# Hybrid RWKV-7 / GLA / SSD stack on one core: modulation weights summed over row tiles by VectorE alone, 1024 columns at a time

## The chip, the cores and the metric

The kernel runs on one core of a Trainium2 chip. The metric is device time in microseconds (us) of one execution. TensorE (PE) multiplies matrices into PSUM, VectorE (DVE) does elementwise work on two sources, ScalarE (ACT) does activations and copies, GpSimd (POOL) and SyncE (SP) mostly issue DMAs. Each engine takes its instructions in the order in which they stand in its queue, and they wait for each other through semaphores.

## The reference

Four layers (RWKV-7, GLA, SSD, RWKV-7) act on 256 tokens of width 2048, in float32. Each layer has a modulation: a vector-matrix product of `silu(c)` (2048) with a 2048 x 6144 matrix, whose result is split into shift, scale and gate. The change touches only how this product is computed.

```python
c_act = jax.nn.silu(c)
for i in range(DEPTH):                                   # DEPTH = 4, kinds 0, 1, 2, 0
    mod = jnp.einsum('bd,de->be', c_act, ada_w[i]) + ada_b[i]
    shift, scale, gate = jnp.split(mod[:, None, :], 3, axis=-1)
    h = rms_normalize(x, norm_g[i], NORM_EPS) * (1 + scale) + shift
    out = mixer(h)                                       # rwkv7_mixer, gla_mixer or ssd_mixer
    x = x + (gate * out)
return rms_normalize(x, final_g, NORM_EPS)
```

The four matrices `ada_w` are 201 MB in float32, and each element is used once.

## The kernel before, in words

**The projections.** All large matrix products go through `jobs` (L333). A job is one weight tile `raw` of 128 x 1024 float32 (512 KB: 4 row tiles of 256 columns), loaded by SP's queue. ScalarE casts it to a rounded part H (L312), VectorE subtracts to get the rest L (L314), and TensorE does 24 matmuls of 128 x 256 with them (L367). There are 6 `raw` buffers, 3 of H and 3 of L. The program has 706 such tiles.

**The modulation.** It runs beside the projections, as a Python generator (`ada_all`, L227) that is advanced a step at a time. A step of `ada_group` (L259) loads one 512 KB tile of `ada_w` (two row tiles of 512 columns) into the same six `raw` buffers. There are 8 steps to a group, 4 groups to a third (shift, scale or gate) and 3 thirds to a layer: 384 steps. A group needs, for its 512 columns, the sum over 2048 rows of `c_act[row] * w[row, column]`. It is formed in two ways at once: a step whose flag in `share` is 1 is multiplied by TensorE (L277, eight matmuls per step, each 32 identical columns of `c_act` against 128 columns, at four places of the array), and a step whose flag is 0 is added by VectorE into `adaacc`, one instruction per row tile of 512 columns (L283; the first one is ScalarE's, L281). At the group's end, matmuls with ones (L287) sum `adaacc` over its 128 partitions on top of that, and a copy and a small matmul (L290, L291) turn the row into a column. `SHARE` gives TensorE 4 steps of 8, `FEW` 2, `LEAST` 1; layers set the pattern as they go.

**When the steps come.** The 64 steps of layer 0's shift and scale come first, since nothing can start without them. After that `tick` (L369) is called after each job and advances the generator to where `PACE` says, at most 2 steps at a time, and not while `hold` is set (from the last columns of a layer's output projection into the next layer). Where a layer needs a third that is not done, `ada_need` (L299) advances the generator until it is.

**What sets the order.** A scheduler sorts each engine's instructions when the program is built, by priority and a model of time; the queues then run in that fixed order. SP's queue issues nearly all weight tiles, of `ada_w` and of the projections, in one order.

Of the kernel before, what the change touches and what calls it, by code (L numbers as in the profile page):

```python
# [9 lines left out]
F32 = mybir.dt.float32  # L10
# [3 lines left out]
ALU = mybir.AluOpType  # L14

P = 128
D = 2048
T = 256
DT = D // P
# [75 lines left out]

PACE = ((0, 120, 316, 484, 620), (0, 96, 240, 288, 320))

SHARE = (1, 0, 1, 0, 1, 0, 1, 0)
FEW = (1, 0, 0, 0, 1, 0, 0, 0)
LEAST = (1, 0, 0, 0, 0, 0, 0, 0)  # L100

# [30 lines left out]
class Kern:  # L132
    def __init__(self, ctx, tc, A, out, layers=(0, 1, 2, 3), final=True):
# [15 lines left out]
        self.hold = False  # L149
        self.share = SHARE  # L150
        self.par = self.const.tile([P, NPAR], F32, name="par")
# [75 lines left out]
    def ada_all(self):  # L227


        for i in self.layers:  # L230
# [8 lines left out]
            for q in range(3):  # L239
                if (i, q) in self.mods:  # L240
                    continue
                for n in range(4):
                    yield from self.ada_group(i, q, n, ms[q])
                if q == 1:
                    self.norm_gain(i, ms[q], 0, DT)
                self.mods[(i, q)] = ms[q]
# [12 lines left out]
    def ada_group(self, i, q, n, m):  # L259

        nc = self.nc
        wv = Weights((0, 512, self.A["ada_w"][i]))
        n0 = q * D + n * 512
        kc = RAWC // 512
        ps = acc = None
        share = self.share
        for b in range(DT // kc):
            raw = self.wpool.tile([P, kc, 512], F32, name="raw")
            nc.sync.dma_start(out=raw, in_=wv(kc * b, kc, n0, 512))
            for u in range(kc):  # L270
                k = kc * b + u
                if share[b]:
                    start = ps is None
# [5 lines left out]
                elif acc is None:  # L279
                    acc = self.adap.tile([P, 512], F32, name="adaacc")  # L280
                    nc.scalar.mul(out=acc, in_=raw[:, u, :], mul=self.cact[:, k:k + 1])  # L281
                else:
                    nc.vector.scalar_tensor_tensor(out=acc, in0=raw[:, u, :], scalar=self.cact[:, k:k + 1], in1=acc,  # L283
                                                   op0=ALU.mult, op1=ALU.add)
            yield
        for e in range(4 if acc is not None else 0):
            nc.tensor.matmul(ps[32 * e:32 * e + 32, 0:P], self.c("one", 0, 1).broadcast_to([P, 32]),  # L287
                             acc[:, e * P:(e + 1) * P], start=False, stop=True)
        s = self.adap.tile([P, P], F32, name="adas")
        nc.scalar.copy(out=s, in_=ps[:, 0:P])  # L290
        nc.tensor.matmul(ps[:, P:P + 4], s, self.c("sel4"), start=True, stop=True)  # L291
        nc.vector.tensor_tensor(out=m[:, 4 * n:4 * n + 4], in0=ps[:, P:P + 4],
                                in1=self.p("ada_b", 48 * i + 16 * q + 4 * n, 4), op=ALU.add)

    def ada_tick(self, n=1):
# [205 lines left out]
    def _rwkv(self, i, j):  # L501
# [130 lines left out]
        nc.gpsimd.dma_start(out=x[:, :, 1:], in_=xd)  # L632
        if i != self.layers[-1]:
            self.share = LEAST
        def ev(jj, ps):
# [6 lines left out]
        with ExitStack() as ctx:  # L642
            nb, = self.banks(ctx, f"pn{i}", nb=2)
            self.share = FEW if i != self.layers[-1] else SHARE
            un = 0
# [120 lines left out]
    def rwkv_second(self, i, j, un, spill, kept, rb, last):  # L766
# [110 lines left out]
        rs = self.rsqrt_tiny(mu, 1.0 / H, GN_EPS, rb)  # L877
        Y = rb.tile([P, 8, H], F32, name="Y")
        nc.vector.tensor_tensor(out=Y, in0=y8, in1=rs.unsqueeze(2).broadcast_to([P, 8, H]), op=ALU.mult)
# [150 lines left out]
    def _gla(self, i, ctx):  # L1030
# [3 lines left out]
        C, NCH = 64, 4  # L1034
        self.share = FEW
        hs = self.norm_parts(i)
# [172 lines left out]
    def _ssd(self, i):  # L1209
# [3 lines left out]
        NH, C = 64, 128  # L1213
        self.share = SHARE
        hs = self.norm_parts(i)
# [46 lines left out]
    def ssd_group(self, g, hs, win, acd, tk, due):  # L1262
# [66 lines left out]
        nc.tensor.matmul(ps, bk, xd.rearrange("p h d -> p (h d)"), start=True, stop=True)  # L1329
        st = su.tile([P, 8, 64], F32, name="st", bufs=1)  # L1330
        nc.scalar.copy(out=st.rearrange("p h d -> p (h d)"), in_=ps)
# [72 lines left out]
def host_inputs(inp):  # L1404
    w = {n: np.asarray(a) for n, a in inp.items()}
    a = {n: blocks(w[n], T, 4) for n in ("rwkv_w_in", "rwkv_w_out", "gla_w_out", "ssd_w_out")}
    a["ada_w"] = blocks(w["ada_w"], 512, 2)
    for n in ("rwkv_dec_w1", "rwkv_iclr_w1"):
# [32 lines left out]
```

## Time and profile before

| what | value |
|---|---|
| median of 3 runs | 2909.22 us (2904.7 to 2921.3) |
| the profiled execution | 2918.82 us |
| its span, first to last instruction | 2916.8 us |
| PE busy | 2782.8 us (95%) |
| DVE busy | 2116.8 us (73%) |
| ACT busy | 1397.7 us (48%) |
| DMA | 673.82 MB, mean 231 GB/s |
| mean granted clock of TensorE | 0.963 |

A busy time is the union of an engine's instructions, waits excluded. The rows further below cut the span into stretches: 0 to 146 us is the start (layer 0's shift and scale, and its first projection); 146 to 511 us the rest of the value projection, the key projection and most of the receptance projection of layer 0; 511 to 736 us its gate projection, with the state update running beside it; 736 to 890 us its output projection; 890 to 1409 us the GLA layer; 1409 to 2117 us the SSD layer, cut at 1522 us; 2117 to 2917 us the last RWKV layer and the end. The cuts are read from when L314 works on which weights.

### The profile page before, as it was taken

What the parts mean: (1) busy time and instruction counts of PE and PEld (TensorE: products, weight loads), DVE (VectorE), ACT (ScalarE), POOL (GpSimd) and SP (SyncE); (2) the same over time, 40 slices, a digit from 0 to 9 for tenths busy, and PEclk for the clock granted to TensorE, in tenths of its full rate; (3) what the DMA queues carried; (4) which work ended last, traced back from release to release, by engine and by line L of the source; (5) the groups of instructions that cost most, each with busy time, mean ns of one, the idle gap of its engine ahead of it and who ended that gap; (6) DMA issues with size and microseconds to landing.
All of it is one profiled execution on the core that took longest, in us unless ns stands there. A gap on an engine that the chain in (4) does not pass through costs nothing.

```text
span 2916.8 us, 66210 instructions
## 1 busy us (share of the span) xinstructions
PE 2782.8 (95%) x27138; PEld 2584.9 (89%) x27138; DVE 2116.8 (73%) x4000; ACT 1397.7 (48%) x2355; POOL 154.2 (5%) x298
## 2 busy tenths in 40 slices
PE   6889999999999999998999999999889999999997
PEld 4789888989898899997999999999779989899997
DVE  5778876667787867777888786887577876565675
ACT  3465564423335543444654454544357656442333
POOL 0010110100100000000000000000001111010010
PEclk8899899999999999999999999999999988999999
DMA  9877768866775777876876666666556765675553
GB/s 349 299 271 259 240 215 276 297 223 224 237 268 195 265 259 273 291 261 211 292 253 222 223 219 222 217 204 223 169 171 222 229 183 176 198 275 172 168 178 112
DMA packets 239135, 673.82 MB, mean 231 GB/s; under 512 B 72272, under 2 KB 78416, under 8 KB 235760
## 3 DMA queue, kind: packets, MB, share of 16 engines
q1 hardware_dynamic: 217904, 580.84, 60.0%
q0 software_dynamic: 20928, 88.75, 8.6%
q8 instruction: 213, 3.49, 0.5%
q14 instruction: 90, 0.74, 0.1%
HBM read 620.66 MB, written 48.82 MB: 230 GB/s over the span
## 4 chain that ended last, share of the span: by engine, by line
PE 76%; DMA 5%; DVE 5%; issue 1%; ACT 1%; SPq 1%; POOL 0%; DVEq 0%; ACTq 0%; POOLq 0%
PE acc L367 58%; PE g L762 2%; PE mx L277 2%; DMA raw<-in_ada_w 2%; DMA rv<-rd 1%; DVE L L314 1%; PE b L869 1%; PE b L846 1%; PE b L868 1%; PE b L841 1%; PE b L791 1%; DMA sp<-yd 1%; PE b L694 1%; PE b L996 1%; PE b L982 1%
## 5 line engine op out<-in xcount | busy, mean ns | idle before, releaser
L367 PE MATMUL acc<-xs,H 128*128 128x256 f32 x8480 | 1640.3, 291 | 16.7 <-ACT xs L382 6.4
L367 PEld LDWEIGHTS acc<-xs,H 128*128 128x128 f32 x8480 | 1355.3, 195 | 59.8 <-issue 21.5
L367 PE MATMUL acc<-xs,L 128*128 128x256 f32 x4240 | 1226.5, 290 | 8.6 <-DVE L L314 8.6
L312 ACT CAST H<-raw 128x1024 fp32r<-128x1024 f32 (+1 forms) x706 | 718.5, 1018 | 947.3 <-PE acc L367 688.8
L314 DVE TENSOR_TENSOR L<-raw,H 128x1024 fp32r<-128x1024 f32 (+1 forms) x706 | 835.8, 1185 | 339.4 <-ACT H L312 321.7
L367 PEld LDWEIGHTS acc<-xs,L 128*128 128x128 f32 x4240 | 824.9, 195 | 22.1 <-DVE L L314 10.2
L283 DVE SCALAR_TENSOR_TENSOR adaacc<-raw,cact,adaacc 128x512 f32<-128x512 f32 x418 | 312.5, 748 | 133.7 <-DMA raw<-in_ada_w 118.3
L367 PE MATMUL acc<-ys,H 128*128 128x256 f32 x1536 | 290.3, 288 | 2.7 <-ACT ys L382 1.9
L367 PEld LDWEIGHTS acc<-ys,H 128*128 128x128 f32 x1536 | 240.8, 192 | 14.4 <-issue 10.2
L367 PE MATMUL acc<-ys,L 128*128 128x256 f32 x768 | 219.2, 286 | 0.0
L367 PEld LDWEIGHTS acc<-ys,L 128*128 128x128 f32 x768 | 146.5, 191 | 3.2 <-issue 3.2
L277 PE MATMUL mx<-raw,cact 128*32 128x128 f32 x2416 | 115.4, 295 | 15.6 <-DMA raw<-in_ada_w 14.9
L405 DVE SCALAR_TENSOR_TENSOR x<-acc,mod,x 128x256 f32<-128x256 f32 x192 | 84.2, 480 | 52.3 <-PE acc L367 51.8
L525 ACT ACTIVATE hn<-x,mod,omu 128x256 f32<-128x256 f32 x192 | 113.0, 599 | 4.0 <-DVE xm L528 2.6
L277 PEld LDWEIGHTS mx<-raw,cact 128*32 128x32 f32 x2416 | 64.7, 114 | 42.5 <-DMA raw<-in_ada_w 13.0
L367 PE MATMUL acc<-H,xs 128*128 128x256 f32 x512 | 97.3, 290 | 0.0
L528 DVE SCALAR_TENSOR_TENSOR xm<-x,par,hn 128x256 f32<-128x256 f32 x192 | 88.3, 478 | 1.3 <-ACT hn L525 0.3
L367 PEld LDWEIGHTS acc<-H,xs 128*128 128x128 f32 x512 | 82.4, 197 | 1.2 <-issue 1.2
L762 PE MATMUL g<-abkp 64*128 64x128 f32 x768 | 72.0, 296 | 2.8 <-DVE abkp L784 2.6
L367 PE MATMUL acc<-L,xs 128*128 128x256 f32 x256 | 73.6, 289 | 0.0
L762 PEld LDWEIGHTS g<-abkp 64*128 64x128 f32 x768 | 55.0, 189 | 17.6 <-issue 8.2
L1257 DVE SCALAR_TENSOR_TENSOR cva<-cvp,hcw,cva 128x256 f32<-128x256 f32 x144 | 64.8, 480 | 0.0
(350 smaller groups left out, 3182.3 us busy)
## 6 DMA issues: line engine op xcount, KB each, us to landing
raw<-in_ada_w SPq DMA_DIRECT2D x384, 512.0 KB, 5.0
raw<-in_rwkv_w_in SPq DMA_DIRECT2D x256, 512.0 KB, 4.9
raw<-in_ssd_w_in SPq DMA_DIRECT2D x128, 512.0 KB, 4.6
raw<-in_gla_w_in SPq DMA_DIRECT2D x96, 512.0 KB, 4.7
raw<-in_ssd_w_out SPq DMA_DIRECT2D x64, 512.0 KB, 4.1
raw<-in_rwkv_w_out SPq DMA_DIRECT2D x48, 512.0 KB, 3.8
abkp<-kd POOLq DMA_DIRECT2D x16, 1024.0 KB, 7.3
raw<-in_gla_w_out SPq DMA_DIRECT2D x32, 512.0 KB, 4.9
```

Source lines behind the costliest of these rows:

```text
L277: nc.tensor.matmul(ps[32 * e:32 * e + 32, 0:P], self.cact[:, k:k + 1].broadcast_to([P, 32]), raw[:, u, e * P:(e + 1) * P], start=start, st ...
L283: nc.vector.scalar_tensor_tensor(out=acc, in0=raw[:, u, :], scalar=self.cact[:, k:k + 1], in1=acc, op0=ALU.mult, op1=ALU.add)
L312: nc.scalar.copy(out=hi, in_=raw[:, a:a + n])
L314: nc.vector.tensor_tensor(out=lo, in0=raw[:, a:a + n], in1=hi, op=ALU.subtract)
L367: self.nc.tensor.matmul(ps, lhs, rhs, start=first and part == 0 and w is hi, stop=last and w is lo)
L405: nc.vector.scalar_tensor_tensor(out=self.x[:, t, 1:], in0=ps[:, u, :], scalar=gate[:, t:t + 1], in1=self.x[:, t, 1:], op0=ALU.mult, op1=A ...
L525: nc.scalar.activation(t1, x[:, k, 1:], AF.Identity, scale=self.omu[:, col:col + 1], bias=self.mods[(i, 0)][:, k:k + 1])
L528: done[k] = nc.vector.scalar_tensor_tensor(out=xm, in0=x[:, k, 0:T], scalar=self.p("rwkv_mu", col), in1=t1, op0=ALU.mult, op1=ALU.add)
L694: nc.tensor.matmul(ps[:, q * T:(q + 1) * T], w2[0:LORA, n, q * P:(q + 1) * P], lora[nm][0:LORA], start=True, stop=True)
L762: self.nc.tensor.matmul(ps[h][:, n * C:(n + 1) * C], s[r, q, c * C:(c + 1) * C], t[r, q, c * C:(c + 1) * C], start=True, stop=True)
L791: nc.tensor.matmul(ps[:, q * T:(q + 1) * T], self.c("blk"), rT[:, q, :], start=True, stop=True)
L1257: nc.vector.scalar_tensor_tensor(out=a, in0=src[:, k:k + T], scalar=w[k], in1=a, op0=ALU.mult, op1=ALU.add)
```

## The change

Layer 0's shift and scale (64 steps) stay as they were, always with the pattern `SHARE`. The other ten thirds go through a new function, `ada_third`. It takes 1024 columns at a time, so a third is 2 halves instead of 4 groups. A step is still one 512 KB tile, now one row tile of 1024 columns. All 16 row tiles are added into a 128 x 1024 `adaacc`: the first by ScalarE, the other 15 by VectorE, one instruction each. TensorE only sums the result over partitions, once per 1024 columns, with four matmuls of 256 columns. `FEW` and `LEAST` are gone. The tile is loaded one step before ScalarE's first use of it. `PACE` has new points: no step between tick 0 and tick 60, 16 steps by tick 78, 96 by tick 150, and about the old pace from tick 319 on. Two small buffers are shared with others (`Y = s8`, `st = xd`). The matrices lie in memory in the new order of tiles.

```diff
-PACE = ((0, 120, 316, 484, 620), (0, 96, 240, 288, 320))
+PACE = ((0, 60, 78, 150, 319, 530, 660), (0, 0, 16, 96, 234, 292, 320))
 SHARE = (1, 0, 1, 0, 1, 0, 1, 0)
-FEW = (1, 0, 0, 0, 1, 0, 0, 0)
-LEAST = (1, 0, 0, 0, 0, 0, 0, 0)
...
-                for n in range(4):
-                    yield from self.ada_group(i, q, n, ms[q])
+                yield from self.ada_third(i, q, ms[q])
...
+    def ada_third(self, i, q, m):
+        nc = self.nc
+        for g in range(2):
+            acc = self.adap.tile([P, 1024], F32, name="adaacc")
+            for k in range(DT):
+                raw = self.wpool.tile([P, RAWC], F32, name="raw")
+                nc.sync.dma_start(out=raw, in_=self.A["ada_w"][3 * i + q - 2, g, k])
+                if k == 0:
+                    yield
+                    nc.scalar.mul(out=acc, in_=raw, mul=self.cact[:, k:k + 1])
+                else:
+                    nc.vector.scalar_tensor_tensor(out=acc, in0=raw, scalar=self.cact[:, k:k + 1], in1=acc,
+                                                   op0=ALU.mult, op1=ALU.add)
+                if 0 < k < DT - 1:
+                    yield
+            ps = self.bank()
+            for e in range(4):
+                nc.tensor.matmul(ps[32 * e:32 * e + 32, 0:T], self.c("one", 0, 1).broadcast_to([P, 32]),
+                                 acc[:, e * T:(e + 1) * T], start=True, stop=True)
+            s = self.adap.tile([P, T], F32, name="adas")
+            nc.scalar.copy(out=s, in_=ps[:, 0:T])
+            ps = self.bank()
+            for j in range(2):
+                nc.tensor.matmul(ps[:, j:j + 7:2], s[:, j * P:(j + 1) * P], self.c("sel4"), start=True, stop=True)
+            nc.vector.tensor_tensor(out=m[:, 8 * g:8 * g + 8], in0=ps[:, 0:8],
+                                    in1=self.p("ada_b", 48 * i + 16 * q + 8 * g, 8), op=ALU.add)
+            yield
...
-        Y = rb.tile([P, 8, H], F32, name="Y")
+        Y = s8
...
-        st = su.tile([P, 8, 64], F32, name="st", bufs=1)
+        st = xd
...
-    a["ada_w"] = blocks(w["ada_w"], 512, 2)
+    a["ada_w0"] = blocks(w["ada_w"][0:1, :, :2 * D], 512, 2)
+    n = w["ada_w"].shape[0]
+    thirds = w["ada_w"].reshape(n, D, 3, D).transpose(0, 2, 1, 3).reshape(3 * n, D, D)[2:]
+    a["ada_w"] = blocks(thirds, 1024, 1)
```

Two places in the built programs show what moves. Line numbers in the second rows of each pair are those of the changed kernel: its L298 is the load of `ada_w` (L269 before), L304 the VectorE addition (L283), L340 the cast's rest (L314), L348 the load of projection weights (L322), L431 the residual update (L405).

SP's queue at the end of layer 0's output projection, before the change; `in_gla_low` is the first tile of the next layer:

```order
L322 DMA raw<-in_rwkv_w_out 128x512
L269 DMA raw<-in_ada_w 128x1024
L322 DMA raw<-in_rwkv_w_out 128x512 x2
L269 DMA raw<-in_ada_w 128x1024
L322 DMA raw<-in_rwkv_w_out 128x512
L269 DMA raw<-in_ada_w 128x1024
L322 DMA raw<-in_rwkv_w_out 128x512
L269 DMA raw<-in_ada_w 128x1024
L322 DMA raw<-in_rwkv_w_out 128x512 x2
L322 DMA raw<-in_gla_low 128x4x16
```

The same place of the same queue after the change:

```order
L348 DMA raw<-in_rwkv_w_out 128x512
L298 DMA raw<-in_ada_w 128x1024
L348 DMA raw<-in_rwkv_w_out 128x512
L298 DMA raw<-in_ada_w 128x1024 x2
L348 DMA raw<-in_rwkv_w_out 128x512
L298 DMA raw<-in_ada_w 128x1024
L348 DMA raw<-in_rwkv_w_out 128x512
L298 DMA raw<-in_ada_w 128x1024
L348 DMA raw<-in_rwkv_w_out 128x512
L298 DMA raw<-in_ada_w 128x1024 x8
L348 DMA raw<-in_gla_low 128x4x16
```

Eight tiles of `ada_w` now stand in one piece between the last weights of layer 0 and the first of layer 1. Over the whole output projection (from its first weight row to `in_gla_low`) there are 29 tiles of `ada_w` before and 52 after, beside 40 of its own in both.

VectorE at the end of the same stretch before the change, from the last residual updates (L405) to the start of the norm (L1012 to L1020, the inverse root of the mean square):

```order
L405 SCALAR_TENSOR_TENSOR x<-acc,mod_2_88,x 128x256 x2
L314 TENSOR_TENSOR L<-raw,H 128x1024
L405 SCALAR_TENSOR_TENSOR x<-acc,mod_2_88,x 128x256 x2
L321 MEMSET raw 128x4x112
L314 TENSOR_TENSOR L<-raw,H 128x1024
L1012 TENSOR_SCALAR rsv<-nb 128x2
L1013 TENSOR_SCALAR rst<-rsv 128x2
L1015 TENSOR_SCALAR rsr<-rst 128x2
L1018 TENSOR_TENSOR rst<-rsr 128x2
L1019 SCALAR_TENSOR_TENSOR rst<-rst,rsv 128x2
```

The same place on VectorE after the change, where the norm is L1035 to L1043:

```order
L304 SCALAR_TENSOR_TENSOR adaacc<-raw,cact,adaacc 128x1024
L431 SCALAR_TENSOR_TENSOR x<-acc,mod_2_88,x 128x256 x2
L304 SCALAR_TENSOR_TENSOR adaacc<-raw,cact,adaacc 128x1024 x2
L1035 TENSOR_SCALAR rsv<-nb 128x2
L304 SCALAR_TENSOR_TENSOR adaacc<-raw,cact,adaacc 128x1024
L1036 TENSOR_SCALAR rst<-rsv 128x2
L304 SCALAR_TENSOR_TENSOR adaacc<-raw,cact,adaacc 128x1024
L347 MEMSET raw 128x4x112
L1038 TENSOR_SCALAR rsr<-rst 128x2
L304 SCALAR_TENSOR_TENSOR adaacc<-raw,cact,adaacc 128x1024
L1041 TENSOR_TENSOR rst<-rsr 128x2
```

The steps of the norm, which stood next to each other, now stand between additions that each wait for a tile to land.

## Rows read from the trace of the kernel before

**Rows 1.** Page: busy time of each engine, share of the span, instructions
```profile
PE 2782.8 (95%) x27138; PEld 2584.9 (89%) x27138; DVE 2116.8 (73%) x4000; ACT 1397.7 (48%) x2355; POOL 154.2 (5%) x298
```

**Rows 2.** Windows by stage: length, then busy us (instructions) of PE, PEld, DVE, ACT, POOL
```profile
146.00:511.00 365.00, 346.46 (x4382) 316.72 (x4375) 276.33 (x557) 212.66 (x404) 39.13 (x78) 0.95 0.76 252
511.00:736.00 225.00, 221.62 (x2063) 204.50 (x2062) 149.44 (x279) 80.22 (x137) 22.19 (x41) 0.97 0.72 250
736.00:890.00 154.00, 148.68 (x1326) 136.90 (x1324) 123.09 (x235) 58.56 (x101) 10.21 (x19) 0.99 0.74 243
890.00:1409.00 519.00, 497.93 (x4238) 459.01 (x4241) 382.40 (x629) 246.94 (x378) 2.18 (x4) 0.97 0.74 252
1409.00:1522.00 113.00, 113.00 (x1071) 105.24 (x1072) 96.63 (x192) 59.46 (x92) 1.06 (x2) 1.00 0.79 276
1522.00:2117.00 595.00, 586.89 (x5187) 562.92 (x5186) 446.01 (x826) 282.37 (x409) 5.10 (x9) 0.99 0.65 214
2117.00:2917.00 800.00, 758.89 (x7818) 711.03 (x7816) 547.72 (x1095) 394.52 (x716) 74.12 (x142) 0.96 0.59 189
```

**Rows 3.** The same windows, line L277 alone: busy us of PE and PEld
```profile
146.00:511.00 365.00, 22.62 (x440) 11.80 (x432) 0.95 0.76 252
511.00:736.00 225.00, 5.15 (x128) 3.00 (x128) 0.97 0.72 250
736.00:890.00 154.00, 4.90 (x112) 2.75 (x112) 0.99 0.74 243
890.00:1409.00 519.00, 19.49 (x436) 10.93 (x440) 0.97 0.74 252
1409.00:1522.00 113.00, 7.75 (x160) 3.99 (x160) 1.00 0.79 276
1522.00:2117.00 595.00, 17.97 (x416) 10.23 (x416) 0.99 0.65 214
2117.00:2917.00 800.00, 12.64 (x224) 6.51 (x224) 0.96 0.59 189
```

**Rows 4.** PE's timeline around one step on L277: start, duration, count
```profile
1103.40 0.28 PE L367 MATMUL acc<-L,xs 128*128 128x256 f32 x1
1103.61 0.64 PE L277 MATMUL mx<-raw,cact 128*32 128x128 f32 x16
1104.18 0.50 PE L367 MATMUL acc<-H,xs 128*128 128x256 f32 x2
```

**Rows 5.** Groups on VectorE: count | busy us, mean ns | idle before, its releasers
```profile
L314 DVE TENSOR_TENSOR L<-raw,H 128x1024 fp32r<-128x1024 f32 (+1 forms) x706 | 835.8, 1185 | 339.4 <-ACT H L312 321.7 <-PE acc L367 5.5 <-PE pv L367 4.2
L283 DVE SCALAR_TENSOR_TENSOR adaacc<-raw,cact,adaacc 128x512 f32<-128x512 f32 x418 | 312.5, 748 | 133.7 <-DMA raw<-in_ada_w 118.3 <-ACT adaacc L281 11.6
L1257 DVE SCALAR_TENSOR_TENSOR cva<-cvp,hcw,cva 128x256 f32<-128x256 f32 x144 | 64.8, 480 | 0.0
```

**Rows 6.** Windows by stage, line L283 alone: busy us of DVE
```profile
146.00:511.00 365.00, 37.68 (x51) 0.95 0.76 252
511.00:736.00 225.00, 31.41 (x42) 0.97 0.72 250
736.00:890.00 154.00, 27.55 (x37) 0.99 0.74 243
890.00:1409.00 519.00, 109.37 (x146) 0.97 0.74 252
1409.00:1522.00 113.00, 14.23 (x19) 1.00 0.79 276
1522.00:2117.00 595.00, 32.96 (x44) 0.99 0.65 214
2117.00:2917.00 800.00, 18.62 (x25) 0.96 0.59 189
```

**Rows 7.** Short windows, as rows 2; last come granted clock, DMA share, GB/s
```profile
850.00:860.00 10.00, 10.00 (x89) 9.67 (x89) 8.86 (x15) 4.13 (x6) 0.00 (x0) 1.00 0.97 342
...
890.00:900.00 10.00, 4.95 (x19) 3.75 (x19) 6.73 (x26) 3.00 (x8) 0.00 (x0) 0.59 0.35 107
```

More of the change, by code (lines that the diff above doesn't have):

```diff
@@ L149, in __init__ @@
         self.hold = False
-        self.share = SHARE
         self.par = self.const.tile([P, NPAR], F32, name="par")
@@ L261, in ada_group @@
         nc = self.nc
-        wv = Weights((0, 512, self.A["ada_w"][i]))
+        wv = Weights((0, 512, self.A["ada_w0"][i]))
         n0 = q * D + n * 512
@@ L265, in ada_group @@
         ps = acc = None
-        share = self.share
         for b in range(DT // kc):
@@ L271, in ada_group @@
                 k = kc * b + u
-                if share[b]:
+                if SHARE[b]:
                     start = ps is None
@@ L279, in ada_group @@
                 elif acc is None:
-                    acc = self.adap.tile([P, 512], F32, name="adaacc")
+                    acc = self.adap.tile([P, 1024], F32, name="adaacc")[:, 0:512]
                     nc.scalar.mul(out=acc, in_=raw[:, u, :], mul=self.cact[:, k:k + 1])
@@ L288, in ada_group @@
                              acc[:, e * P:(e + 1) * P], start=False, stop=True)
-        s = self.adap.tile([P, P], F32, name="adas")
+        s = self.adap.tile([P, T], F32, name="adas")[:, 0:P]
         nc.scalar.copy(out=s, in_=ps[:, 0:P])
@@ L632, in _rwkv @@
         nc.gpsimd.dma_start(out=x[:, :, 1:], in_=xd)
-        if i != self.layers[-1]:
-            self.share = LEAST
         def ev(jj, ps):
@@ L643, in _rwkv @@
             nb, = self.banks(ctx, f"pn{i}", nb=2)
-            self.share = FEW if i != self.layers[-1] else SHARE
             un = 0
@@ L1034, in _gla @@
         C, NCH = 64, 4
-        self.share = FEW
         hs = self.norm_parts(i)
@@ L1213, in _ssd @@
         NH, C = 64, 128
-        self.share = SHARE
         hs = self.norm_parts(i)
```

## The prediction

> **What bounds the kernel now.** I read the page's busy times first: PE 2782.8 us, 95% of the span, DVE 2116.8 us, 73% [rows 1]. So the kernel runs as fast as TensorE is fed, but with an average of 73% VectorE can be the limit in some stretch. Next I read the windows by stage [rows 2]. PE is busy for the whole of 1409 to 1522 us, and for 587 of the 595 us after it. It has gaps of 18.5 us in 146 to 511, 21 us in the GLA layer, and 41 us in the last layer. DVE's share is 76% in the first of these stages, 80% from 736 to 890, and 86% from 1409 to 1522. The chain of waits runs mostly over PE's L367, the projections. The timeline of PE at one step on L277 comes next [rows 4], to learn whether the part that is removed takes time or only fills gaps. Last come the groups on VectorE, for durations and for what it waits for [rows 5].
>
> **What is removed from PE.** All of L277 after layer 0's shift and scale. Its busy time in the seven stages is 22.6, 5.2, 4.9, 19.5, 7.8, 18.0 and 12.6 us, together 90.5 us for 1904 records [rows 3], 47.5 ns each. Does a step really push the projection back by 16 x 47.5 ns = 0.76 us? In the timeline the L matmul starts at 1103.40 and the next H pair at 1104.18 [rows 4], 0.78 us later; this pair takes 0.50 us. A matmul of 128x256 follows its neighbour by about 0.12 us (256 columns at the 2.4 GHz of granted clock 1.00), so the step cost about 0.66 us to the start of the pair and a tenth more inside it. I take 90.5 us as the whole credit, to be had where PE is the limit.
>
> The Trainium skill, "Perfetto Trace Analysis", section "Identifying the Most-Contended Engine", calls TensorE's matmul busy time a bad measure, since matmuls are pipelined, and wants weight-load time. By that rule L277 is worth the PEld column of the same windows, 49.2 us, and the forecast below would be 41 us less of a gain. The trace doesn't agree here: 0.66 us and more for 16 records is 41 ns each at least, where the weight loads give 49.2 us / 1904 = 26 ns.
>
> The matmuls with ones keep their number of columns (20 groups of 1024 instead of 40 of 512), so nothing is credited there. ScalarE loses 40 first products of 512 columns and gets 20 of 1024: nothing, on an engine that is 48% busy.
>
> **What is added to DVE.** The new instruction, 128x1024 on two sources with a per-partition scalar, isn't in the trace. The same operation takes 480 ns at 256 columns and 748 ns at 512 [rows 5], so 748 + 2 x 268 = 1284 ns at 1024. The bounds are L314's mean of 1185 ns, which mixes in narrower forms, and twice 748 ns, 1496 ns. With 300 of them the bounds shift DVE by -30 and +64 us. I take 1284 ns, which two rows of the same operation give. Counted in the built order between the same L314 rows, the seven stages hold 8 (and 4 old ones), 37, 45, 115, 23, 45 and 27 wide instructions, where 51, 42, 37, 146, 19, 44 and 25 narrow ones stood [rows 6]. That changes DVE by -24.4, +16.1, +30.2, +38.3, +15.3, +24.8 and +16.1 us, +116 us in all, which makes it 252, 166, 153, 421, 112, 471 and 564 us against stages of 365, 225, 154, 519, 113, 595 and 800 us [rows 2]. So two stages are full: 736 to 890 and 1409 to 1522.
>
> **How much of DVE's idle time can be used.** DVE is idle for 800 us, and for 321.7 us of it L314 waits for ScalarE's H [rows 5]. I take these 40% as idle time that stays, and the rest as usable. A stage then lasts as long as the longer of two: its old time less L277, or DVE's new time plus 40% of its old idle time.
>
> - **146 to 511**, credit 22.6 us. The pace holds the steps back until tick 60, so DVE loses 24 us and DMA about 40 tiles. Some of the 18.5 us of gaps goes too; what is late next there is the chain of small instructions of the state's preparation. I take 4 us of it (bounds 7 us of loss and 18.5 us of gain): -26.
> - **511 to 736**, 5.2 us. DVE 166 + 30 = 196 us of 220. With 37 tiles for 25 on the queues: -4.
> - **736 to 890**, 4.9 us. DVE 153.3 + 0.4 x 30.9 = 165.7 us: +12, PE's credit is lost. The queue carries 52 tiles of `ada_w` for 29; 23 x 0.524 MB on top of 243 GB/s x 154 us is 49.5 MB, 145 us at the 342 GB/s that 850 to 860 us shows [rows 7], so DMA stays just under it. Behind it stand the eight tiles that shift and scale of layer 1 still lack: 4.2 MB, 12.3 us at that rate. Queued behind them are `in_gla_low` on SP, and on DVE the steps of the norm, for which the whole next layer waits. PE is already half idle there, 4.95 of 10 us, at a mean granted clock of 0.59 [rows 7], so part of the landing hides behind the norm: I take 4 us of 0 to 12.3. Together +16 (bounds -5 and +42).
> - **890 to 1409**, 19.5 us. DVE 421 + 55 = 476 of 500 us. The first jobs of the layer catch up with two steps each, 2 x 15/16 x 1.28 = 2.4 us of DVE beside 1.2 us for L, more than a job's 24 x 0.12 = 2.9 us on PE. I give a third of the credit back: -13.
> - **1409 to 1522**, 7.8 us. DVE 111.9 + 6.6 = 118.5 us, the credit is lost: +6 (bounds -8 and +14).
> - **1522 to 2117**, 18.0 us. DVE 471 + 60 = 531 of 577 us; a third back, since the group's own additions come in bursts: -12.
> - **2117 to 2917**, 12.6 us. DVE 564 + 101 of 787 us; PE has gaps of its own in this stage: -9.
>
> The shared buffers: `ysq` and `xd` are written again only a unit or a group later, long after their last reader; nothing.
>
> The sum is -26 - 4 + 16 - 13 + 6 - 12 - 9 = **-42 us**. The profiled execution took 2918.8 us, 2.0 us more than its span, and 9.6 us more than the median of the runs. 2918.8 - 42 = 2877, and at the median **2867 us**, 1.4% less.
>
> **Rivals.**
>
> *VectorE hides all of it.* All seven credits and the 4 us: -94.5, 2815 us. For it: in 850 to 860 DVE is 89% busy and PE 100% [rows 7]. Against it: two stages in which DVE would have to work at 99%.
>
> *The end of layer 0 is bound by DMA.* If the queues keep the 243 GB/s that this stage has on average, its 49.5 MB take 204 us, +50, and the eight tiles 12 us more: +62 where I have +16, so +4 in all and 2913 us. For it: DMA is at a share of 0.97 in 850 to 860 with fewer tiles. Against it: the same row, 342 GB/s.
>
> *The weight-load reading is right.* Then 41 us less are removed: 2908 us.
>
> *VectorE becomes the bound (slower).* If DVE's idle time is nearly all waiting that stays, the stages grow by what is added. With 90% of it staying, DVE sets 234, 181, 544, 127 and 605 us from 511 to 2117: +8.5, +27 with 4 for the landing, +25, +14 and +10; with -26 and -9 at the ends that is +53, 2962 us. The point is at about 80%: below it PE's credit wins. For it: L314 stands in order behind these longer instructions, and PE behind L314. Against it: three buffers of L, some 8.6 us of PE's work, and PE at 100% beside a DVE of 86%.
>
> **Chances.** Forecast 0.55, with 2845 to 2890 as its own range; all hidden 0.18; DMA at layer 0's end 0.14; weight loads 0.04; VectorE 0.09. A difference of 0.5%, about 15 us, is what a measurement of this kernel can tell from none: the limits are 2895 and 2924 us. Faster: 0.55, 0.18 and a little of the others, 0.75. Within: most of the DMA and weight-load cases, 0.16. Slower: 0.09. For 8 in 10 the range goes from 2820 to 2916: it leaves out the lower half of the second case, the last one, and the upper end of the DMA case.
>
> **What would show it.** PE busy down by about 90 us, to 2690. DVE up by about 116 us, to 2233, and the wide instruction at 1.28 us; at 1.4 us or more the two full stages grow further. The stage of 365 us shorter by about 26 us. Layer 0's output projection 16 us longer, with DVE close to 100% and PE waiting for L314 or for tiles. In the SSD layer after the first 113 us, PE still at 98% or more; if it is at 95% there, the last rival is at work. The forecast is wrong if PE's busy time doesn't fall by the 90 us, or if its gaps grow by more than some 70 us.

## The result, and the profile after

The changed kernel takes 2883.27 us (median of 4 runs, 2881.41 to 2885.51) beside 2915.26 us for the kernel before on the same chip: a ratio of 0.9893, 95% interval 0.9855 to 0.9931. On another occasion it took 2884.42 us (6 runs) beside 2914.53 us, ratio 0.9904 (0.9875 to 0.9933). The forecast of 2867 us has the sign right, and the time lies in its range, 16 us above it: 6 of these 16 us are the median of the kernel before (2909 us in the runs shown first, 2915 us beside this result), 10 are gain that was forecast (42 us) and not found (32 us).

The profiled execution went from a span of 2916.8 us to 2879.4 us, -37.4. The page's line of busy times after the change answers to [rows 1]:

```profile
PE 2691.4 (93%) x25074; PEld 2533.2 (88%) x25074; DVE 2213.7 (77%) x3918; ACT 1392.7 (48%) x2315; POOL 153.8 (5%) x298
```

TensorE has 91.4 us less to do and VectorE 96.8 us more. The span gave up only 37.4 of the 91.4 us: TensorE's idle time grew by 54 us. Where that is can be read from the windows by stage after the change (same columns as [rows 2]; the cuts are again where L340, once L314, turns to other weights):

```profile
145.00:478.00 333.00, 316.44 (x3765) 301.07 (x3762) 250.91 (x508) 207.08 (x392) 39.05 (x78) 0.94 0.63 201
478.00:664.00 186.00, 182.78 (x1805) 172.75 (x1806) 151.01 (x237) 74.11 (x120) 20.46 (x38) 1.00 0.88 317
664.00:871.00 207.00, 177.44 (x1448) 160.63 (x1446) 163.50 (x282) 65.79 (x115) 11.76 (x22) 0.95 0.72 244
871.00:1384.00 513.00, 485.50 (x3789) 453.05 (x3790) 418.32 (x577) 246.34 (x366) 1.65 (x3) 0.96 0.78 272
1384.00:1502.00 118.00, 107.12 (x849) 103.65 (x848) 105.30 (x185) 56.95 (x84) 1.06 (x2) 0.93 0.81 285
1502.00:2092.00 590.00, 572.91 (x4779) 555.11 (x4778) 466.19 (x847) 285.65 (x409) 5.58 (x10) 0.98 0.64 212
2092.00:2879.00 787.00, 742.67 (x7578) 700.37 (x7576) 562.93 (x1095) 393.80 (x712) 74.04 (x142) 0.97 0.58 192
```

The second and third stage have to be taken together: the schedule now casts the output projection's weights ahead of the gate projection's matmuls, so the cut at 664 us has less of TensorE's work ahead of it than the old one at 736 us.

| stage of before (us) | before | after | change | predicted | change in the second profile |
|---|---|---|---|---|---|
| 146 to 511 | 365 | 333 | -32 | -26 | -27 |
| 511 to 890 | 379 | 393 | +14 | +12 | +19 |
| 890 to 1409 | 519 | 513 | -6 | -13 | -3 |
| 1409 to 1522 | 113 | 118 | +5 | +6 | +4 |
| 1522 to 2117 | 595 | 590 | -5 | -12 | -6 |
| 2117 to the end | 800 | 787 | -13 | -9 | -14 |

The last column is the changed kernel's profile from the other occasion (span 2888.7 us), cut at the same weights: 483, 880.8, 1396.7, 1514 and 2103 us.

VectorE's groups after the change, as [rows 5]:

```profile
L340 DVE TENSOR_TENSOR L<-raw,H 128x1024 fp32r<-128x1024 f32 (+1 forms) x706 | 834.1, 1184 | 249.0 <-ACT H L338 233.9 <-PE acc L393 5.0 <-PE pv L393 2.7
...
L304 DVE SCALAR_TENSOR_TENSOR adaacc<-raw,cact,adaacc 128x1024 f32<-128x1024 f32 x300 | 384.0, 1280 | 111.5 <-DMA raw<-in_ada_w 109.5 <-ACT adaacc L302 0.5
```

The wide addition takes 1280 ns (1284 were predicted). L waits 234 us for H where it waited 322 us: the part that the prediction took for idle time that stays did shrink, but by less than the rest.

For the experiments I cut the span where a layer really begins, at the last step of its first norm: 893.6, 1366.1 and 2141.0 us before the change. (The stage cut at 1409 us lies 43 us inside the SSD layer.) The rows are layer 0 from 145 us on, the GLA layer, the SSD layer, and the last layer with the end; before the change:

```profile
145.00:893.60 748.60, 718.50 (x7784) 659.41 (x7782) 551.22 (x1082) 351.82 (x642) 71.53 (x138) 0.96 0.74 250
893.60:1366.10 472.50, 456.06 (x3910) 420.69 (x3910) 343.58 (x534) 217.31 (x329) 0.52 (x1) 0.98 0.75 258
1366.10:2141.00 774.90, 761.31 (x6726) 723.24 (x6726) 592.26 (x1123) 379.96 (x559) 10.62 (x17) 0.99 0.67 221
2141.00:2916.80 775.80, 738.59 (x7664) 693.75 (x7664) 534.79 (x1070) 385.65 (x701) 71.33 (x138) 0.96 0.59 189
```

and after it:

```profile
145.00:874.60 729.60, 678.76 (x7026) 635.61 (x7022) 568.90 (x1036) 349.31 (x627) 71.27 (x138) 0.96 0.72 243
874.60:1339.30 464.70, 442.23 (x3474) 412.73 (x3474) 374.45 (x497) 216.74 (x318) 0.52 (x1) 0.97 0.80 279
1339.30:2116.00 776.70, 741.54 (x6078) 715.25 (x6078) 624.81 (x1124) 378.79 (x549) 10.59 (x17) 0.97 0.66 222
2116.00:2879.40 763.40, 722.34 (x7424) 683.05 (x7424) 549.99 (x1070) 384.89 (x697) 71.21 (x138) 0.97 0.58 192
```

Layer by layer that is -19.0, -7.8, +1.8 and -12.4 us (-9.2, -5.1, +0.5 and -14.3 us in the second profile). The SSD layer has 19.8 us less of matmuls and is not shorter: its idle TensorE time (length less PE) rose from 13.6 to 35.2 us.

### The profile page after: what moved, and what is told of

Read it like the earlier page. It is cut to its first block, busy times and chain, and to the rows that moved or that the text cites. A ratio compares the mean times of both kernels' runs of the same rounds, so it can differ in the third digit from the quotient of the medians.

```text
span 2879.4 us, 62022 instructions
## 1 busy us (share of the span) xinstructions
PE 2691.4 (93%) x25074; PEld 2533.2 (88%) x25074; DVE 2213.7 (77%) x3918; ACT 1392.7 (48%) x2315; POOL 153.8 (5%) x298
## 4 chain that ended last, share of the span: by engine, by line
PE 72%; DVE 10%; DMA 10%; issue 3%; ACT 2%; SPq 2%; POOL 0%; DVEq 0%; ACTq 0%; POOLq 0%
PE acc L393 56%; DMA raw<-in_ada_w 3%; DVE L L340 3%; PE g L785 2%; PE pv L393 2%; DVE adaacc L304 2%; ACT H L338 1%; DMA raw<-in_rwkv_w_in 1%; DMA raw<-in_rwkv_w_out 1%; DMA dx<-bd 1%; PE b L892 1%; PE b L869 1%; DMA raw<-in_gla_w_in 1%; PE b L891 1%; PE b L864 1%
## 5 line engine op out<-in xcount | busy, mean ns | idle before, releaser
L340 DVE TENSOR_TENSOR L<-raw,H 128x1024 fp32r<-128x1024 f32 (+1 forms) x706 | 834.1, 1184 | 249.0 <-ACT H L338 233.9
L304 DVE SCALAR_TENSOR_TENSOR adaacc<-raw,cact,adaacc 128x1024 f32<-128x1024 f32 x300 | 384.0, 1280 | 111.5 <-DMA raw<-in_ada_w 109.5
L431 DVE SCALAR_TENSOR_TENSOR x<-acc,mod,x 128x256 f32<-128x256 f32 x192 | 83.7, 478 | 33.3 <-PE acc L393 33.1
L408 ACT CAST xs<-xm 128x256 fp32r<-128x256 f32 x128 | 50.9, 400 | 34.1 <-DVE xm L554 31.8
L278 DVE SCALAR_TENSOR_TENSOR adaacc<-raw,cact,adaacc 128x512 f32<-128x512 f32 x56 | 42.0, 749 | 28.1 <-DMA raw<-in_ada_w 23.4
```

The source lines that it names most:

```text
L304: nc.vector.scalar_tensor_tensor(out=acc, in0=raw, scalar=self.cact[:, k:k + 1], in1=acc, op0=ALU.mult, op1=ALU.add)
L340: nc.vector.tensor_tensor(out=lo, in0=raw[:, a:a + n], in1=hi, op=ALU.subtract)
L408: nc.scalar.copy(out=t[:, 0, :], in_=src)
L431: nc.vector.scalar_tensor_tensor(out=self.x[:, t, 1:], in0=ps[:, u, :], scalar=gate[:, t:t + 1], in1=self.x[:, t, 1:], op0=ALU.mult, op1=A ...
```

## The experiments

The theory is that of the prediction: TensorE's credit is real, and VectorE takes part of it back where it is nearly full. Ratios are to the kernel before, run on the same chip.

**The new table of due times.** Two runs take the change apart: the changed kernel with the old table, and the kernel before with the new one.

```diff
-PACE = ((0, 60, 78, 150, 319, 530, 660), (0, 0, 16, 96, 234, 292, 320))
+PACE = ((0, 120, 316, 484, 620), (0, 96, 240, 288, 320))
```

> The changed kernel with the pace points of before, so that steps run from tick 0 and layer 1's shift and scale are done in time. Theory (TensorE's relief is the gain, the late pace costs at the end of layer 0): the output projection of layer 0 carries 29 tiles instead of 52 and nothing stands between the layers; that stretch loses most of its 27 us of idle PE, and the key and receptance projections lose some 12 us to the additions that return there: 2865 to 2885 us, best guess 2875. Rival (the gain is the pace, which frees layer 0's first stages): 2900 us or more.

> The kernel before with only the new pace points; TensorE and VectorE share the steps as before. Theory: the first stages gain some 25 us, the output projection and the layer boundary give most of it back, and TensorE's 90 us stay in: 2900 to 2925 us, best guess 2912. Rival (the pace is the gain): 2885 us.

Both were missed. The wide path with the old table took 2945.51 us, ratio 1.0108 (1.0046 to 1.0169); the new table alone 2958.4 us, 1.0153 (1.0102 to 1.0205). Each half by itself is slower than before, and only both together are faster. The new table's cost to the old arithmetic is spread over all layers (+11, +11, +6 and +7 us in its profile); what carries it stays open. Since that rests on few runs, I ran the first again later, beside the unaltered changed kernel on one chip.

> The changed kernel once more, unaltered, beside the kernel before on another occasion. Theory (the gain is the change's): a ratio of 0.985 to 0.995, about 2885 us beside about 2915. Rival (the first session's four runs were fast ones; the late-pace kernel, which is the same program up to the GLA layer, lost 11 us there): a ratio of 0.997 to 1.005, 2905 to 2930 us.

> The changed kernel with the old table of due times, as in the first such run, now beside the unaltered changed kernel on one chip. Theory (the new table is needed by the wide path): a ratio to before of 1.005 to 1.017, as the first time, and 40 us or more above the unaltered changed kernel. Rival (that run was a slow occasion): within 10 us of the unaltered changed kernel.

The changed kernel gave 0.9904 again, so the gain isn't one of the occasion. With the old table it took 2938.48 us, ratio 1.0092 (1.0069 to 1.0116), 54 us above it: the theory of this run holds. The windows of layer 0 and of the last layer show where; first the unaltered kernel of this pair, then the one with the old table:

```profile
145.00:884.40 739.40, 688.06 (x7022) 645.26 (x7022) 570.49 (x1036) 349.29 (x627) 71.25 (x138) 0.94 0.70 239
...
2127.20:2888.70 761.50, 722.73 (x7424) 683.12 (x7424) 549.46 (x1070) 384.89 (x697) 71.24 (x138) 0.96 0.58 193
```

```profile
145.00:916.90 771.90, 707.74 (x7068) 659.28 (x7066) 588.67 (x1052) 352.60 (x629) 71.12 (x138) 0.93 0.72 243
...
2156.30:2937.00 780.70, 733.79 (x7424) 693.74 (x7424) 548.83 (x1070) 385.08 (x697) 71.46 (x138) 0.95 0.57 188
```

The old table costs 32 us in layer 0 and 19 us in the last layer, and nothing in the two between (465.4 and 774.0 us against 467.4 and 775.4). In layer 0 it puts wide additions into the first stretch, beside the preparation of the state, and VectorE then stands longer in front of tiles that have not landed. VectorE's waits in layer 0, unaltered and with the old table (us, times, longest):

```profile
DVE adaacc L304 <- DMA raw<-in_ada_w: 28.1, 21, 4.5
```

```profile
DVE adaacc L304 <- DMA raw<-in_ada_w: 64.3, 51, 5.1
```

TensorE's idle time there is 64.2 us instead of 51.3. The rest of the 32 us, some 20, is more busy time: the granted clock is lower (0.927 against 0.940 over the layer) and the layer has 46 more matmul records; the two weren't told apart.

**Other tables.** One spread the steps from tick 40 on, one finished the GLA layer's share sooner; from tick 290 on they are the same.

```diff
-PACE = ((0, 60, 78, 150, 319, 530, 660), (0, 0, 16, 96, 234, 292, 320))
+PACE = ((0, 40, 136, 290, 340, 512, 632), (0, 0, 98, 200, 232, 292, 320))             # spread
+PACE = ((0, 60, 78, 150, 290, 340, 512, 632), (0, 0, 16, 96, 200, 232, 292, 320))     # late
```

> The changed kernel with steps from tick 40 on at one per job, so that layer 1's shift and scale are done before layer 0 ends, and a flatter pace through the GLA layer into the SSD layer. Theory A (the end of layer 0 costs because the steps come late): the output projection has its old 29 or so tiles, layer 0 ends 15 us earlier and the start of the SSD layer gains 5: 2862 us, 2850 to 2875. Theory B (additions that run beside layer 0's state preparation, where VectorE has chains of its own, cost more than those at its end, as the old pace showed): layer 0 ends 5 to 20 us later than in the changed kernel: 2885 to 2900 us.

> The changed kernel with its own points up to tick 150 and the flatter pace of e5_spread_pace after it, so that 20 fewer tiles come in the GLA layer and at the start of the SSD layer, and more later. Theory (VectorE is full at the start of the SSD layer): layer 0 as it is, GLA and SSD together 5 to 15 us less: 2873 us, 2865 to 2882. Rival (the additions cost the same wherever they stand): 2883 us.

Both were missed by far: 2939.53 us, ratio 1.0051 (1.0028 to 1.0075), and 2931.67 us, 1.0043 (1.0016 to 1.007). The late table, which leaves layer 0's program as it is, by layer:

```profile
145.00:885.90 740.90, 685.00 (x7022) 642.32 (x7022) 569.72 (x1037) 349.57 (x627) 71.49 (x138) 0.95 0.71 240
...
1359.20:2157.90 798.70, 744.65 (x6090) 714.72 (x6090) 637.06 (x1138) 380.60 (x551) 10.58 (x17) 0.97 0.67 224
2157.90:2938.60 780.70, 727.72 (x7424) 686.96 (x7424) 544.18 (x1066) 384.13 (x697) 71.34 (x138) 0.96 0.57 185
```

Layer 0 agrees with the second run of the changed kernel (739.4). The SSD layer is 22 us longer than with the unaltered table and the last one 17 to 19 us. In the SSD layer the late table has 87 wide additions where the changed kernel has 75, VectorE stands twice as long in front of tiles that have not landed (92.0 us; 46.7 in the changed kernel), and TensorE now waits for L, for which it waited 1.8 us there:

```profile
DVE adaacc L304 <- DMA raw<-in_ada_w: 92.0, 52, 3.9
...
PE acc L393 <- DVE L L340: 16.0, 16, 2.7
```

The spread table's SSD layer is alike (87 additions, 95.2 us). Over the whole span VectorE's wait in front of these tiles is 178 to 223 us in the four profiles with the old, the spread and the late table, and 110 and 121 us in the two of the changed kernel. So these tables are slow together with more waiting for tiles; whether the wait is what makes them slow, no run shows by itself. For the last layer the record has less: read in the same way, the last layer of the wide kernels took 781 to 783 us in the four profiles with tables that end at tick 620 or 632, and 761 to 772 us in the profiles of the changed kernel and of its variants with full additions and the table that ends at 660, but for the one with matmuls put back. Why some 30 ticks weigh that much there stays open (VectorE has 23 to 28 wide additions there in the late, the old and the spread table, 27 in the changed kernel).

**TensorE's side.** 120 of the wide steps get eight matmuls of 128 columns back, whose result nobody reads:

```diff
+                if k in (1, 4, 7, 9, 12, 14):
+                    if k == 1:
+                        side = self.bank()
+                    for e in range(8):
+                        nc.tensor.matmul(side[32 * (e % 4):32 * (e % 4) + 32, 0:P],
+                                         self.cact[:, k:k + 1].broadcast_to([P, 32]), raw[:, e * P:(e + 1) * P],
+                                         start=k == 1 and e < 4, stop=k == 14 and e > 3)
```

> The changed kernel, and beside it TensorE again does eight matmuls of 128 columns on 6 of 16 tiles, 120 steps where 119 were removed, into a bank that nobody reads. Theory (a step costs the projections 0.76 us wherever PE is the limit, 91 us in all): 50 to 80 us more than the changed kernel, best guess 2945 us. Rival (weight loads, 49 us, or gaps that are filled): at most 30 us more, 2913 us or less.

It took 2991.49 us, ratio 1.0261 (1.0216 to 1.0305): 108 us above the changed kernel (107 by the ratios), more than expected. Their group:

```profile
L310 PE MATMUL mx<-raw,cact 128*32 128x128 f32 x1920 | 95.1, 283 | 15.0 <-DMA raw<-in_ada_w 14.7 <-DVE mod L324 0.3
L310 PEld LDWEIGHTS mx<-raw,cact 128*32 128x32 f32 x1920 | 50.9, 109 | 38.4 <-DMA raw<-in_ada_w 16.5 <-issue 2.0 <-DVE adaacc L304 0.8
```

1920 records for 95.1 us of busy time, as the 1904 removed ones had 90.5 us [rows 3], and the whole of it is on the path: TensorE's busy time is 2798.6 us, 107.2 more than in the changed kernel, and its idle time is 184.7 us beside 188.0. Next to none of the idle time took the matmuls in, not even in the SSD layer, where 23.8 us of them were put back and the idle time went from 35.2 to 30.6 us. The Trainium skill, "Perfetto Trace Analysis", section "Identifying the Most-Contended Engine", judges how close TensorE is to its roofline by the share of peak FLOPs and the share of weight loads, not by matmul busy time. Taken as a price for single matmuls, which is the prediction's step and not the page's, that would be 50.9 us here; the time grew by twice as much.

**VectorE's side.** One kernel leaves out the 300 wide additions (the ten thirds are then computed from their first row tile alone; all tiles are still loaded), another makes each of them two of 512 columns.

```diff
-                    nc.vector.scalar_tensor_tensor(out=acc, in0=raw, scalar=self.cact[:, k:k + 1], in1=acc,
-                                                   op0=ALU.mult, op1=ALU.add)
+                    pass                                                                   # left out
+                    for s in (slice(0, 512), slice(512, 1024)):                            # or narrow
+                        nc.vector.scalar_tensor_tensor(out=acc[:, s], in0=raw[:, s], scalar=self.cact[:, k:k + 1],
+                                                       in1=acc[:, s], op0=ALU.mult, op1=ALU.add)
```

> The changed kernel without VectorE's 300 wide additions: all tiles are loaded, only the first of each half is used, so the modulation is not the reference's. Theory (VectorE's additions cost at layer 0's end, at the start of the SSD layer and a little elsewhere, about 40 us): 2830 to 2860 us, best guess 2843. Rival 1 (the end of layer 0 is bound by its tiles on the DMA queues): that stretch stays as long as it is, and the time is 2865 us or more. Rival 2 (VectorE costs nothing, since it is off the path): 2880 us.

> The changed kernel with each wide addition as two of 512 columns: the same columns in twice the instructions, 300 x (2 x 0.749 - 1.280) = 65 us more of VectorE. Theory (what costs is VectorE's time): 300 wide ones cost 68 us for 384 us, so 10 to 25 us more: 2898 us. Rival (what costs is the width, since a short instruction of the norm or an L waits behind 1.28 us): 5 to 20 us less, 2870 us.

Without the additions: 2815.2 us, ratio 0.9658 (0.9616 to 0.97). That this is the figure of the prediction's rival "VectorE hides all of it", 2815 us, is luck in part: the kernel before took 2915 us beside it and not 2909, so the gain is 100 us where the rival had 94.5. It is about what the change would have brought if the additions cost nothing. They do cost 68 us, together with the waits for their tiles on VectorE and with what the tiles cost by staying in the buffers, since this kernel has neither. Two layers of that kernel, GLA and SSD:

```profile
860.70:1314.60 453.90, 441.71 (x3486) 412.62 (x3486) 251.82 (x395) 219.24 (x323) 0.52 (x1) 0.97 0.82 288
1314.60:2057.20 742.60, 728.95 (x6078) 705.95 (x6078) 545.91 (x1050) 374.05 (x549) 10.61 (x17) 0.98 0.68 233
```

The SSD layer loses 34 us with 79 us less of VectorE's work, the GLA layer 11 us with 123 us less. TensorE's idle time falls to 14 us in the SSD layer and 12 us in the GLA layer, where it was 14 and 16 us before the change; the other 13 of the SSD layer's 34 us are busy time of the same 6078 records. So the additions' price isn't spread by their time: the layer with less of it pays three times as much.

The narrow form was expected at 2898 us if VectorE's time counts; it took 2921.2 us, ratio 1.0005 (0.9981 to 1.003), the whole gain gone:

```profile
L305 DVE SCALAR_TENSOR_TENSOR adaacc<-raw,cact,adaacc 128x512 f32<-128x512 f32 x600 | 426.8, 747 | 152.8 <-DMA raw<-in_ada_w 152.2
```

42.8 us more of busy time (426.8 against 384.0) cost about 30 us by the ratios, 0.7 us each. Leaving all 384 us out had given 0.18 us each. So VectorE's time looks much dearer at the margin than on average. That isn't shown: the 300 more instructions may cost something by themselves, and VectorE's wait for these tiles grew too (152.2 us, from 110 and 121), and neither was tried apart. What the run does show is that halving the instruction's length didn't help, so the rival that puts the price on the width of one instruction is out.

**The wait for tiles, and the end of layer 0.** Is it the additions or the wait in front of them? One kernel uses every tile one step of the walk after its load.

```diff
                 nc.sync.dma_start(out=raw, in_=self.A["ada_w"][3 * i + q - 2, g, k])
+                yield
                 if k == 0:
-                    yield
...
-                if 0 < k < DT - 1:
-                    yield
...
-            yield
```

> The changed kernel with every weight tile of the wide path used one step of the walk later than its load is issued. Theory (VectorE stands in order behind tiles that have not landed, 109 us of waits at L304, and the chains behind it hold TensorE up): 10 to 25 us less than the unaltered changed kernel of this call, most of it in layer 0 and the SSD layer. Rival (what the additions cost TensorE is their time on VectorE, 384 us, not the wait for tiles): within 6 us of it, with VectorE's wait at L304 gone or halved.

It took 2887.95 us, ratio 0.9921 (0.9904 to 0.9938), within 4 us of the unaltered kernel on that chip. VectorE's whole wait at this line, of the unaltered kernel and of this one:

```profile
DVE adaacc L304 <- DMA raw<-in_ada_w: 121.0, 91, 8.8
```

```profile
DVE adaacc L303 <- DMA raw<-in_ada_w: 115.5, 83, 6.6
```

The wait hardly moved: the later use didn't take it away, so this run can't say what the wait costs. The time is what the rival expected, but not for a reason that the run shows.

At layer 0's end the change leaves additions between the steps of the norm, as its order showed. The last kernel moves the table's points 4 to 9 ticks ahead in layer 0, and with that these tiles away from there.

```diff
-PACE = ((0, 60, 78, 150, 319, 530, 660), (0, 0, 16, 96, 234, 292, 320))
+PACE = ((0, 56, 74, 141, 319, 530, 660), (0, 0, 16, 96, 234, 292, 320))
```

> The changed kernel with the points of the new table 4 to 9 ticks earlier in layer 0 (0 until tick 56, 16 by 74, 96 by 141), so that no tile of the modulation stands between the last weights of layer 0 and the first of layer 1. Theory (the additions that stand between the steps of the norm there cost about 9 us): TensorE's idle time in the last 20 us before layer 0's end falls from 12.6 us to 4 to 6 us, and the time is 5 to 12 us below the two medians of the changed kernel (2883 and 2884): 2872 to 2879, a ratio of 0.983 to 0.988. Rival (an addition costs the same wherever it stands, since VectorE is full from 664 us on): the idle time at the end goes, as much comes earlier in the layer, and the ratio is 0.988 to 0.993.

It took 2894.54 us, ratio 0.9922 (0.9894 to 0.995), no less than the changed kernel (0.9893 and 0.9904): the rival. The windows of 20 us ahead of layer 0's end, before the change (one), after it (two), with the earlier points (two) and without the additions (one):

```profile
873.60:893.60 20.00, 16.27 (x134) 11.63 (x132) 16.50 (x41) 10.21 (x24) 0.00 (x0) 0.95 0.72 221
```

```profile
834.60:854.60 20.00, 16.79 (x113) 11.64 (x111) 16.87 (x29) 9.27 (x20) 0.00 (x0) 1.00 0.83 268
854.60:874.60 20.00, 7.45 (x40) 4.02 (x40) 18.47 (x34) 6.73 (x12) 0.00 (x0) 0.72 0.90 294
```

```profile
849.60:869.60 20.00, 9.46 (x56) 7.87 (x55) 15.41 (x23) 5.52 (x10) 0.00 (x0) 0.66 0.79 268
869.60:889.60 20.00, 15.42 (x108) 10.81 (x108) 15.42 (x40) 11.47 (x24) 0.00 (x0) 0.97 0.55 163
```

```profile
840.70:860.70 20.00, 15.68 (x102) 10.14 (x100) 11.91 (x35) 8.23 (x20) 0.00 (x0) 0.97 0.99 370
```

In the last 20 us TensorE's idle time went from 3.7 us before the change to 12.6 us after it, and fell back to 4.6 us with the earlier points, as the theory had it. But 10.5 us now stand in the 20 us ahead of that (3.2 us in the changed kernel): moved, not saved. Over the whole of layer 0 TensorE's idle time is 57.4 us with the earlier points, beside 50.8 and 51.3 us in the changed kernel. TensorE's longest wait in that kernel's last 80 us of the layer, 6.7 us, is behind another chain of small instructions, the group norm of the state's output (L902).

Without the additions all tiles still stand in the queue in front of the next layer, DMA is at a share of 0.99, and TensorE's idle time is 4.3 us. So the rate at which these tiles land isn't what costs at this place; the additions are, with the buffers that they keep.

**The shared buffers.** The kernel before with `Y = s8` and `st = xd` alone:

```diff
-        Y = rb.tile([P, 8, H], F32, name="Y")
+        Y = s8
...
-        st = su.tile([P, 8, 64], F32, name="st", bufs=1)
+        st = xd
```

> The kernel before with the two shared buffers of the change alone (Y = s8, st = xd). Theory: each is written again only a unit or a group later, so nothing: 2905 to 2925 us. Rival (the next unit's square waits for the transposes of this one): some 24 units of 1 us or more, 2935 us.

2916.5 us, ratio 0.9993 (0.9963 to 1.0024): nothing, as predicted.

## Why the prediction was nearly right

**The removed matmuls.** Right in size, and not too high in price: TensorE's busy time fell by 91.4 us (90.5 predicted; its windows hold 1916 records, 12 of them still of layer 0's shift and scale, which is under 1 us), and putting as many back cost 108 us. The rival that goes by weight loads is out.

**The added VectorE time.** The instruction's size is right (1280 ns), and the additions' own time rose by 113.5 us (384.0 and 42.0 for the 56 narrow ones that are left, where 312.5 stood). VectorE's busy time rose by 96.8 us only. About 10 us of the difference are a matter of counting, since a busy time is the union of instructions that overlap a little at their ends; the rest is that other small instructions are fewer or shorter.

**How much of VectorE's idle time can be used.** This is the step that failed in size. That 40% of VectorE's idle time stays and the rest can be used fills two stages and says that the others have room. Its sums come near for layer 0 (+14 and +19 from 511 to 890 where +12 was predicted) and for 1409 to 1522 (+5 and +4, predicted +6). In the GLA layer and from 1522 to 2117 a third of the credit was to be given back, and it was over two thirds: -6 and -5 in place of -13 and -12, or -3 and -6 in the second profile. These 14 to 16 us are the error. In the first profile the first stretch and the last gave 10 of them back by gaining more than predicted, so the sum is off by 5 only (-37.4 against -42): that is luck, and in the second profile the sum is -28.

The rule behind it fails too, in that a stage lasts as long as the longer of TensorE's and VectorE's time. If it held, matmuls put back where VectorE's time is the longer would be hidden in part. The run had next to none of them hidden (107 us, with TensorE's idle time as it was), so here the two add. TensorE's waits in the SSD layer show why. Before the change, its longest wait behind one of the small instructions of VectorE and ScalarE:

```profile
PE b L457 <- DVE xm L454: 9.4, 2, 5.2
```

After it, in the same layer:

```profile
PE b L483 <- DVE xm L480: 12.0, 2, 7.6
PE acc L393 <- DVE cvt L1374: 7.1, 3, 3.2
PE b L1342 <- DVE xT L1281: 6.4, 2, 3.7
PE acc L393 <- ACT cvp L1294: 4.6, 2, 3.1
```

L itself is hardly among them (1.8 us). What comes late are the convolution (cvt, cvp), the transposed input (xT) and the norm's diagonal (xm): chains of short instructions that go back and forth between engines, each step of which now may find a 1.28 us addition ahead of it. VectorE is 80% busy in this layer, not full, and TensorE waits all the same; without the additions these waits are gone but for xm (7.1 us).

The addition's length is not all that such a step may find. VectorE takes its queue in order, and if the addition's tile has not landed, the wait for it stands in the chain too. In the norm ahead of the SSD layer, behind which TensorE's longest wait there stands (xm, 7.6 us), one tile came 2.09 us late:

```profile
1334.52 0.16 DVE L1042 SCALAR_TENSOR_TENSOR rst<-rst,rsv 128x2 f32<-128x2 f32 x1
1336.76 1.28 DVE L304 SCALAR_TENSOR_TENSOR adaacc<-raw,cact,adaacc 128x1024 f32<-128x1024 f32 x1 [2.09 <-DMA raw<-in_ada_w]
1337.96 0.15 DVE L1043 SCALAR_TENSOR_TENSOR rsr<-rst,rsr 128x2 f32<-128x2 f32 x1
```

Over the whole SSD layer VectorE's wait for these tiles is 46.7 us, where it was 11.1 us before the change. The kernel without additions takes away both the additions and these waits, and the later use took away neither, so how the 34 us divide between them stays open.

**The end of layer 0.** 4 us were taken of bounds of 0 and 12.3 us, and TensorE's idle time in the last 20 us rose by 8.8: inside the bounds, twice the size. The carrier was half wrong: the prediction gave it to the landing of eight tiles on SP's queue and to the norm on VectorE. It is VectorE alone at this place. VectorE there after the change:

```profile
859.14 2.60 DVE L304 SCALAR_TENSOR_TENSOR adaacc<-raw,cact,adaacc 128x1024 f32<-128x1024 f32 x2
861.65 0.15 DVE L1035 TENSOR_SCALAR rsv<-nb 128x2 f32<-128x2 f32 x1
861.77 1.28 DVE L304 SCALAR_TENSOR_TENSOR adaacc<-raw,cact,adaacc 128x1024 f32<-128x1024 f32 x1
862.97 0.16 DVE L1036 TENSOR_SCALAR rst<-rsv 128x2 int32<-128x2 int32 x1
```

No idle time is noted in front of any of these additions: the tiles have landed, unlike what the built order was taken to mean, and each step of the norm waits for the addition ahead of it. TensorE's longest wait of the layer ends there:

```profile
PE mx L310 <- DVE rsr L1043: 9.6, 1, 9.6
```

**The first stretch.** -26 was predicted for the credit and for holding the steps back, -32 and -27 measured, and with the old table layer 0 is longer than before the change (771.9 against 748.6 us). That the new table is a condition for the gain, and not only a part of it, was nowhere in the prediction.

**The rivals.** "DMA at layer 0's end" is out by the kernel without additions. "VectorE hides all of it" has the right price and is not what happens. "VectorE becomes the bound" is right that the SSD layer's whole credit is taken back, and wrong in price everywhere and in its carrier: TensorE was to stand behind L, and that wait is 1.8 us in the SSD layer. From 1522 to 2117 TensorE is 97% busy, between the 98% of the forecast and the 95% of this rival.

## What to carry to other kernels

Work taken off the busiest engine was worth its busy time here. What it costs on the engine that takes it over isn't told by that engine's idle share, but by which serial chains stand behind it there. So look for the chains of short instructions that wait for each other across engines, and count what is put between their steps: the long instruction, and the wait for its data. Cutting that instruction in two made it no cheaper. A table of due times belongs to the instructions it was made for: test both parts apart before crediting either.

## What the runs showed that was not expected

The same program, run twice, differed by 9.8 us in layer 0 (729.6 and 739.4 us) with the same idle time of TensorE (50.8 and 51.3 us): its busy time was 678.8 and 688.1 us, at a mean granted clock of 0.957 and 0.940. The later layers differed by 3 us at most. A difference of 10 us between two single profiles is therefore not a finding here, which is why the changed kernel's stages and layers are given from both profiles above.

Beside idle time of TensorE the granted clock can be lower: in the last 20 us of layer 0 TensorE was busy for 7.5 us and the mean granted clock was 0.72, where it was 0.95 at 16.3 us busy before the change. The two levels are 1.2 and 2.4 GHz, and a part of that stretch ran at the lower one. The lower level outlasted the idle time: in the first 9.4 us of the next layer TensorE was busy for 7.25 us, and the granted clock was 0.50 throughout. Idle time and clock don't go together in every stretch, though: from 834.6 to 854.6 us TensorE was idle for 3.2 of 20 us at a granted clock of 1.00.
